# The decode state steps of a hybrid decoder kernel: products on ScalarE and VectorE instead of GpSimd

## The chip, the cores and the metric

The kernel runs on one core of a Trainium2 chip. The metric is the device time of one execution in microseconds (us), the median of several runs. The engines have short names in the profile: PE is TensorE (matrix products), PEld its weight loads, DVE is VectorE, ACT is ScalarE, POOL is GpSimd, and SP is the queue that issues the transfers (DMA).

## What is computed

The reference is one inference step of a two-layer decoder trunk, for a prompt of 1024 tokens and, with the same weights, for 8 samples of one new token each. Layer 0 has dilated attention and a state-space mixer (SSD) side by side, layer 1 is an mLSTM mixer. The change lies in the state-space mixer of the 8 samples, whose state is carried from token to token. For one new token the reference's scan comes down to this:

```python
state = state * exp(dt * a) + (dt * x) outer B      # (sample, head, 64, 128)
y     = sum over the last axis of state * C  +  d_skip * x
```

There are 8 samples, 16 heads, 64 values x per head and 128 state columns; B and C have 128 columns per group of heads. The new state is an output, and y goes on through a gate, a norm and the output projection.

## The kernel before

The kernel is written in a tile framework. The code issues instructions to the engines; the framework builds from it one queue per engine, and puts the semaphores in. The order within a queue follows from the dependences and the framework's own estimate of times, so it isn't always that of the code: in the profile both L840 of a step come before its first L842, and L747 of other work stands between the two L842. Once built, the order is fixed, and each engine works through its queue in order, waiting where it must.

All matrix products of the projections (`proj_c`, the matmuls of L112 into the PSUM tile `pf`) use a split of each float32 operand into a high and a low part: three matmuls for one. The weights arrive as `raw`, ScalarE makes the high part (L90, `wh`), VectorE the low one (L91, `wl`).

The stage around the change is the loop at L994 over the output tiles f of the layer's first projection. For f from 0 to 7 each tile belongs to the gate z, and is made in three column blocks c of 344 tokens: 24 matmuls, then `gate_c` takes the block out of PSUM (L235 a copy on ScalarE, L236 a tanh on ScalarE, L237 the product on VectorE), and it is stored to `zd`.

Two kinds of other work are put between these blocks:

- The prompt's state-space scan, in 16 units (chunk of 128 tokens x group). `ssd_prep` (L726 to L760) loads a tile of decays `sE` (L730) and `ea` (L738), masks `sE` with an affine select on GpSimd (L739), takes eight exponentials of 128x128 on ScalarE (L741) and one of `ea` (L743), makes a product and a transpose in the PSUM tile `pcb` (L745, L746), multiplies `sE` by it on VectorE (L747), copies the transpose to `sbt` on ScalarE (L749), transposes four tiles of x into `pxt` (L752) and scales them twice on VectorE (L758, L759). `ssd_main` makes `py` (L771), `pi` (L775) and `psl` (L777) on TensorE, updates the state on VectorE (L780 to L786) and the output on VectorE (L789) and GpSimd (L791). The PSUM tiles of these steps share a ring of five banks.
- The samples' decode steps, `dss_step(j)` (L829) for j from 0 to 7, one per f, called when the third block of a tile is done (the last ones, and what closes the sum, a little later). A step treats eight of the 64 values x of every head: 128 partitions are 8 samples x 16 heads, and the 1024 columns of the state tile `dst` are 8 values x 128 state columns. It loads the tile (L831), scales eight columns of x by dt on VectorE (L833, `dxd`), and then twice, for four values each: GpSimd makes x times B as one 128x512 product with broadcast operands into `dso` (L839), VectorE makes the new state from the old one (L840), GpSimd multiplies the new state by C into `dso` (L841), and VectorE sums each 128 columns (L842). Then the state is stored (L843).

The tiles `dso`, `gz` (the gate block) and `gth` (its tanh) come from one ring of four buffers. From f = 8 on the loop makes the attention gate, and the norm of the first half of the tokens begins.

Of the kernel before, what the change touches and what calls it, by code (L numbers as in the profile page):

```python
# [8 lines left out]
AF = mybir.ActivationFunctionType  # L9
# [19 lines left out]
def body(ctx, tc, I, O):  # L29
    nc = tc.nc  # L30
    V, A, G, PE = nc.vector, nc.scalar, nc.gpsimd, nc.tensor
    mult, add, sub, mx, mn = ALU.mult, ALU.add, ALU.subtract, ALU.max, ALU.min
# [23 lines left out]
    def S(name, dt=F32):  # L56
        return slab.tile([128, 1040], dt, tag="S", name=name)
# [7 lines left out]
    def SM(name, shape, bufs=2, dt=F32):  # L65
        return cur["sm"].tile(shape, dt, tag=name, name=name, bufs=bufs)
# [7 lines left out]
    def X(name="ax"):  # L74
        return ps.tile([128, 512], F32, tag="ax", name=name, bufs=8 - PS_MM)

    def TMP(name="tmp"):
        return tmpp.tile([128, 520], F32, tag="tmp", name=name)
# [4 lines left out]
    def C(name, shape, src=None, p=None):  # L83
        t = (p or cur["cst"]).tile(shape, F32, name=name)
        if src is not None:
            load(t, src)
        return t
# [27 lines left out]
    class Weights:  # L115
# [8 lines left out]
        def load(self, ahead=1):  # L124
            while len(self.raws) < min(ahead, len(self.srcs)):
                self.raws.append(raw_load(*self.srcs[len(self.raws)]))
# [152 lines left out]
    def conv_sample_act(t, y):  # L279
        A.activation(t, y, AF.Tanh)  # L280
        V.scalar_tensor_tensor(t, t, 1.0, y, add, mult)
        return t
# [212 lines left out]
    for g in range(4):  # L495
        for b in range(2):
            u = {}
# [201 lines left out]
    for f in range(12):  # L699
        w = wq0.next()  # L700
        raw = conv_raw()
        o = S("cout")
# [94 lines left out]
    B_b, C_b = BC_b[:, 0:128], BC_b[:, 128:256]  # L797
    dsc2 = C("dsc2", [128, 4])
# [30 lines left out]
    def dss_step(j):  # L829
        t = S("dst")  # L830
        load(t[:, :1024], I["sst"][:, j * 1024 : j * 1024 + 1024])  # L831
        xd = SM("dxd", [128, 8])
        V.tensor_scalar(xd, x_b[:, j * 8 : j * 8 + 8], dsc2[:, 0:1], None, mult)  # L833
        for u in range(2):
            o = TMP("dso")[:, :512]
            ov = o.rearrange("p (a b) -> p a b", b=128)
            tu = t[:, u * 512 : u * 512 + 512]
            tv = tu.rearrange("p (a b) -> p a b", b=128)
            G.tensor_tensor(ov, xd[:, 4 * u : 4 * u + 4].unsqueeze(2).broadcast_to([128, 4, 128]), B_b.unsqueeze(1).broadcast_to([128, 4, 128]), mult)  # L839
            V.scalar_tensor_tensor(tu, tu, dsc2[:, 1:2], o, mult, add)  # L840
            G.tensor_tensor(ov, tv, C_b.unsqueeze(1).broadcast_to([128, 4, 128]), mult)  # L841
            V.reduce_sum(y_b[:, j * 8 + 4 * u : j * 8 + 4 * u + 4], ov, AX.X)  # L842
        store(O["ssds"][:, j * 1024 : j * 1024 + 1024], t[:, :1024])  # L843

# [16 lines left out]

    dq.append(dss_prep)
    dq.extend(lambda j=j: dss_step(j) for j in range(8))
    dq.extend([dss_fin, dss_load, dss_fin2])

# [128 lines left out]
    for f in range(12):  # L994
# [11 lines left out]
        for c in range(3):  # L1006
            t = TMP("gz")
            c0 = c * CH
            if f >= 8:
                a = TMP("al")  # L1010
# [17 lines left out]
            if c < 2:  # L1028
                o = (f % 2) * 520 + c0
# [485 lines left out]
    for h in range(8):  # L1515
# [3 lines left out]
        for j in range(4):  # L1519
# [20 lines left out]
            o = S("cout")  # L1540
# [11 lines left out]
        for j in range(2):  # L1552
            w = wq1.next()
            t2 = S("msz")
            for c in range(3):
                gate_c(w, xh, xl, c, t2[:, c * CH : (c + 1) * CH])
                if j == 0 and c == 2:
                    t = conv_sample_act(*smp)
# [10 lines left out]
        for c in range(9):  # L1569
            vo_block(hd, c, wv)  # L1570
            if c == 1:
                p = X("pms")
# [291 lines left out]
```

## Time and profile before

| | us |
|---|---|
| median of 3 timed runs | 2150.44 (2147.65 to 2151.25) |
| the profiled execution | 2146.51 |
| its span, first to last instruction | 2144.6 |
| GpSimd busy in the 16 products L839, from 480 to 627 us | 18.9 |
| GpSimd busy in the 16 products L841, from 480 to 627 us | 23.8 |
| VectorE busy in the 16 updates L840 | 16.7 |
| VectorE busy in the 16 sums L842 | 10.9 |

A line of the timeline has the start in us, the length, the engine, the line of the kernel, the operation, the tile it writes and the tiles it reads, the shape, and how many instructions were merged into the line; in brackets stands how long the engine was idle before, and what released it. In the table by stage each row has a stretch of time, its length, the busy time of each engine with the number of instructions, the clock that TensorE was granted (1.00 is full), the share of the DMA engines' time, and GB/s. A releaser is inferred from semaphore events, and a wait for several is put down to the one that came last.

### The profile page before, as it was taken

To read this page: it belongs to the slowest core of one execution; us is meant where nothing else is said; L and a number is where in the kernel's file an instruction comes from. 1 tells how busy PE (TensorE), PEld (TensorE's weight loads), DVE (VectorE), ACT (ScalarE), POOL (GpSimd) and SP (SyncE) were. 2 spreads that over 40 slices of the span, in tenths; PEclk is the share of its full clock that TensorE was granted. 3 is DMA by queue.
4 is the path that set the end of the run, shared out by engine and by line. 5 is a ranking of instruction groups with operands and counts; after the bars stand their busy time and mean duration, and the time that the engine had idled before them with its cause. 6 is when DMAs were issued, how large, how long until landed. Compare 5 with 4: busy or idle time off the path is not lost.

```text
span 2144.6 us, 35154 instructions
## 1 busy us (share of the span) xinstructions
PE 2094.1 (98%) x12926; PEld 1878.8 (88%) x12926; DVE 1346.1 (63%) x3192; ACT 849.8 (40%) x1837; POOL 515.6 (24%) x1036
## 2 busy tenths in 40 slices
PE   7999999998899999999999999999999999999998
PEld 6877788997798899989989899898898998987798
DVE  7444378877877656555458466485664755756844
ACT  5434344544434334433335334253342433433421
POOL 4222100115440002152231421413215223141000
PEclk9999999999999999999999999999999999999999
DMA  4222053325555552411214133132231322406842
GB/s 161 73 73 78 21 155 104 96 92 168 157 187 183 174 173 64 100 31 54 84 40 161 28 100 115 35 129 64 91 125 31 102 94 68 151 22 208 280 164 95
DMA packets 162076, 232.29 MB, mean 108 GB/s; under 512 B 41200, under 2 KB 106976, under 8 KB 161904
## 3 DMA queue, kind: packets, MB, share of 16 engines
q1 hardware_dynamic: 161904, 230.04, 34.2%
q8 instruction: 102, 1.67, 0.3%
q14 instruction: 70, 0.57, 0.1%
HBM read 174.35 MB, written 55.62 MB: 107 GB/s over the span
## 4 chain that ended last, share of the span: by engine, by line
PE 78%; DVE 6%; DMA 3%; POOL 3%; issue 2%; ACT 2%; SPq 0%; POOLq 0%; DVEq 0%; ACTq 0%
PE pf L112 32%; PE pvo L112 16%; PE po L931 14%; PE pq L112 4%; PE mN L112 2%; PE mC L112 2%; PE pS L428 2%; PE pO L487 1%; PE mS L1294 1%; PE pT L470 1%; POOL mCl L91 1%; PE mH L1355 1%; PE mS L1296 1%; DMA mE<-mud 1%; POOL dso L841 1%
## 5 line engine op out<-in xcount | busy, mean ns | idle before, releaser
L112 PE MATMUL pf<-yh,wh 128*128 128x344 f32 x1152 | 370.2, 321 | 0.0
L112 PE MATMUL pf<-yl,wh 128*128 128x344 f32 x1152 | 368.9, 320 | 0.0
L112 PE MATMUL pf<-yh,wl 128*128 128x344 f32 x1152 | 368.5, 320 | 0.0
L91 DVE TENSOR_TENSOR wl<-raw,wh 128x1024 fp32r<-128x1024 f32 x128 | 159.8, 1248 | 148.2 <-ACT wh L90 147.8
L90 ACT CAST wh<-raw 128x1024 fp32r<-128x1024 f32 x128 | 133.9, 1047 | 252.8 <-PE po L931 101.0
L112 PEld LDWEIGHTS pf<-yh,wh 128*128 128x128 f32 x1152 | 216.9, 188 | 1.3 <-ACT craw L242 1.0
L112 PEld LDWEIGHTS pf<-yl,wh 128*128 128x128 f32 x1152 | 216.5, 188 | 0.0
L112 PEld LDWEIGHTS pf<-yh,wl 128*128 128x128 f32 x1152 | 216.4, 188 | 0.0
L112 PE MATMUL pvo<-wvh,yh 128*128 128x512 f32 x512 | 206.0, 402 | 0.0
L112 PE MATMUL pvo<-wvh,yl 128*128 128x512 f32 x512 | 201.9, 394 | 0.0
L112 PE MATMUL pvo<-wvl,yh 128*128 128x512 f32 x512 | 201.8, 394 | 0.0
L112 PE MATMUL pf<-xh,wh 128*128 128x344 f32 x576 | 194.3, 337 | 0.0
L112 PE MATMUL pf<-xl,wh 128*128 128x344 f32 x576 | 187.3, 325 | 0.0
L112 PE MATMUL pf<-xh,wl 128*128 128x344 f32 x576 | 187.3, 325 | 0.0
L1282 DVE TENSOR_SCALAR mx<-mx,mbs,md 128x256 f32<-128x256 f32 x64 | 26.4, 413 | 177.1 <-POOL md L1281 177.1
L250 DVE SCALAR_TENSOR_TENSOR cout<-craw,mcw,cout 128x1024 f32<-128x1024 f32 x96 | 123.0, 1282 | 13.2 <-ACT cout L248 11.7
L931 PE MATMUL po<-oh,wl 128*128 128x512 f32 (+2 forms) x384 | 122.9, 320 | 1.7 <-DVE wl L91 1.6
L931 PE MATMUL po<-oh,wh 128*128 128x512 f32 (+2 forms) x384 | 123.0, 321 | 0.9 <-ACT oh L90 0.9
L931 PE MATMUL po<-ol,wh 128*128 128x512 f32 (+2 forms) x384 | 123.0, 321 | 0.0
L112 PEld LDWEIGHTS pvo<-wvh,yl 128*128 128x128 f32 x512 | 96.1, 188 | 22.3
L112 PEld LDWEIGHTS pf<-xh,wh 128*128 128x128 f32 x576 | 110.1, 191 | 5.8 <-issue 5.4
L112 PEld LDWEIGHTS pvo<-wvh,yh 128*128 128x128 f32 x512 | 96.3, 188 | 20.8 <-issue 1.3
(440 smaller groups left out, 4995.5 us busy)
## 6 DMA issues: line engine op xcount, KB each, us to landing
raw<-in_wo SPq DMA_DIRECT2D x56, 512.0 KB
raw<-in_wq SPq DMA_DIRECT2D x32, 512.0 KB
raw<-in_wvo SPq DMA_DIRECT2D x32, 512.0 KB
dC<-in_mcs SPq DMA_DIRECT2D x32, 512.0 KB
out_mcs<-dC SPq DMA_DIRECT2D x32, 512.0 KB
raw<-in_wf SPq DMA_DIRECT2D x24, 512.0 KB
sE<-acd SPq DMA_DIRECT2D x16, 512.0 KB
raw<-in_wz SPq DMA_DIRECT2D x16, 512.0 KB
```

The source lines that it names most:

```text
L90: A.copy(hi, src)
L91: eng.tensor_tensor(lo, src, hi.bitcast(F32), sub)
L112: PE.matmul(out, l, r, start=i == 0, stop=i == n - 1)
L250: V.scalar_tensor_tensor(o[:, :NP], raw[:, j : j + NP], w4[:, j : j + 1], o[:, :NP], mult, add)
L428: PE.matmul(p[:, :n], qT[g][hs, qs], kT[g][hs, ks], start=True, stop=True)
L470: PE.transpose(pt[:, h * n + k : h * n + k + 128], P[:, k : k + 128], ident)
L487: PE.matmul(po[h * 64 : h * 64 + 64, qs], v, PT[:, h * n + k * 128 : h * n + k * 128 + 128], start=j + k == 0, stop=j == 7 and k == nk - 1)
L841: G.tensor_tensor(ov, tv, C_b.unsqueeze(1).broadcast_to([128, 4, 128]), mult)
L931: PE.matmul(p[:, :m], wt[:, ws], at, start=i == 0 and q == 0, stop=i == nk - 1 and q == 2)
L1282: V.tensor_scalar(x, x, bs[:, 6:7], d[:, 2:3], sub, mult)
L1294: PE.matmul(pS[:, 0:128], hd["k"][j][:, tok], hd["q"][j][:, tok], start=j == 0, stop=j == 1)
L1296: PE.transpose(pS[:, 128 + j * 128 : 256 + j * 128], hd["k"][j][:, tok], ident)
```

## The change

Only `dss_step` changes. The product of x and B is made by ScalarE, by four copies of 128x128 per half: each copies B with a scale per partition, one column of `dxd`. The product with C is made by VectorE in one 128x512 instruction. GpSimd has no part in the step any more. Buffers, loads, the state update, the sums and the store stay.

```diff
         for u in range(2):
             o = TMP("dso")[:, :512]
+            for i in range(4):
+                A.activation(o[:, i * 128 : i * 128 + 128], B_b, AF.Copy, scale=xd[:, 4 * u + i : 4 * u + i + 1])
+            tu = t[:, u * 512 : u * 512 + 512]
+            V.scalar_tensor_tensor(tu, tu, dsc2[:, 1:2], o, mult, add)
             ov = o.rearrange("p (a b) -> p a b", b=128)
-            tu = t[:, u * 512 : u * 512 + 512]
-            tv = tu.rearrange("p (a b) -> p a b", b=128)
-            G.tensor_tensor(ov, xd[:, 4 * u : 4 * u + 4].unsqueeze(2).broadcast_to([128, 4, 128]), B_b.unsqueeze(1).broadcast_to([128, 4, 128]), mult)
-            V.scalar_tensor_tensor(tu, tu, dsc2[:, 1:2], o, mult, add)
-            G.tensor_tensor(ov, tv, C_b.unsqueeze(1).broadcast_to([128, 4, 128]), mult)
+            V.tensor_tensor(ov, tu.rearrange("p (a b) -> p a b", b=128), C_b.unsqueeze(1).broadcast_to([128, 4, 128]), mult)
             V.reduce_sum(y_b[:, j * 8 + 4 * u : j * 8 + 4 * u + 4], ov, AX.X)
```

## The prediction

> **What bounds the kernel now.** I read the page of the profile first, then a table of the stage that holds the changed step (480 to 646 us), then its waits, then the order of time on each engine.
>
> ```profile
> PE 2094.1 (98%) x12926; PEld 1878.8 (88%) x12926; DVE 1346.1 (63%) x3192; ACT 849.8 (40%) x1837; POOL 515.6 (24%) x1036
> ...
> PE 78%; DVE 6%; DMA 3%; POOL 3%; issue 2%; ACT 2%; SPq 0%; POOLq 0%; DVEq 0%; ACTq 0%
> ```
>
> TensorE is the bound. An edit on the three other engines can move the end only where TensorE stands still because of them. So the question is how much TensorE loses in this stage, and to whom. Rows of the table by stage follow (stretch, its length, then the busy time of PE, PEld, DVE, ACT and POOL, the granted clock, the share and rate of DMA):
>
> ```profile
> 480.00:606.00 126.00, 114.57 (x801) 100.83 (x800) 101.91 (x180) 53.74 (x150) 67.72 (x87) 0.95 0.52 169
> ...
> 490.00:495.00 5.00, 4.85 (x39) 4.02 (x40) 5.00 (x12) 2.56 (x9) 1.75 (x4) 1.00 0.38 129
> ...
> 515.00:520.00 5.00, 4.45 (x20) 4.01 (x22) 5.00 (x11) 3.02 (x11) 1.74 (x4) 0.50 0.10 35
> ...
> 537.00:542.00 5.00, 4.79 (x25) 4.17 (x27) 5.00 (x12) 2.38 (x9) 1.28 (x4) 0.66 0.25 96
> ...
> 580.00:586.00 6.00, 4.36 (x19) 3.85 (x19) 6.00 (x13) 2.43 (x8) 2.37 (x4) 0.75 0.27 99
> ...
> 600.00:647.00 47.00, 45.58 (x300) 44.17 (x298) 35.46 (x61) 15.92 (x32) 15.44 (x17) 1.00 0.56 185
> ```
>
> TensorE is idle 126.00 - 114.57 = 11.4 us of the first stretch. The timeline of TensorE names the stops (start, length, instruction, and in brackets the idle time before it and its releaser):
>
> ```profile
> 490.15 0.63 PE L752 MATMUL pxt<-ident,cout 128*128 128x128 f32 x4 [1.69 <-DVE sx L759]
> ...
> 515.55 0.80 PE L745 MATMUL pcb<-cout 128*128 128x128 f32 x2 [3.10 <-ACT sbt L749]
> ...
> 537.17 0.49 PE L745 MATMUL pcb<-cout 128*128 128x128 f32 x2 [2.18 <-ACT sbt L749]
> ...
> 559.73 0.63 PE L752 MATMUL pxt<-ident,cout 128*128 128x128 f32 x4 [0.99 <-DVE sx L759]
> ...
> 580.65 0.49 PE L745 MATMUL pcb<-cout 128*128 128x128 f32 x2 [2.25 <-ACT sbt L749]
> ...
> 582.24 0.63 PE L752 MATMUL pxt<-ident,cout 128*128 128x128 f32 x4 [0.99 <-DVE sx L759]
> ```
>
> That is 11.2 of the 11.4 us. The stops come once per decode step: behind the steps 0, 1, 2, 3 and 4 of the eight. After the longer ones the granted clock drops: to 0.50, 0.66 and 0.75 in the rows above, while it stays at 1.00 after 1.69 us. In those three rows the low clock costs about 4.45 x 0.50 + 4.79 x 0.34 + 4.36 x 0.25 = 2.2 + 1.6 + 1.1 = 4.9 us more. So TensorE loses some 16 us behind five steps, the ceiling of what they can give back. How one step holds it, by step 2:
>
> ```profile
> 528.79 2.44 ACT L741 ACTIVATE sE<-sE,nacum 128x128 f32<-128x128 f32 x8
> ...
> 529.36 0.23 DVE L833 TENSOR_SCALAR dxd<-x_b,dsc 128x8 f32<-128x8 f32 x1
> ...
> 529.76 2.85 POOL L839 TENSOR_TENSOR dso<-dxd,BC_b 128x512 f32<-128x512 f32 x2 [1.63 <-DVE dxd L833]
> ...
> 531.65 2.17 DVE L840 SCALAR_TENSOR_TENSOR dst<-dst,dsc,dso 128x512 f32<-128x512 f32 x2 [0.93 <-POOL dso L839]
> ...
> 533.24 2.96 POOL L841 TENSOR_TENSOR dso<-dst,BC_b 128x512 f32<-128x512 f32 x2 [0.62 <-DVE dst L840]
> ...
> 535.00 0.69 DVE L842 TENSOR_REDUCE y_b<-dso 128x4 f32<-128x512 f32 x1 [1.18 <-POOL dso L841]
> 535.61 1.21 DVE L747 TENSOR_TENSOR sE<-sE,pcb 128x1024 f32<-128x1024 f32 x1
> ...
> 536.74 0.68 DVE L842 TENSOR_REDUCE y_b<-dso 128x4 f32<-128x512 f32 x1
> 536.85 0.27 ACT L749 COPY sbt<-pcb 128x128 f32<-128x128 f32 x1 [2.97 <-DVE sE L747]
> ```
>
> VectorE, in order, waits for GpSimd in the middle of the step. Behind that wait stands the multiplication of sE, behind it ScalarE's copy of sbt, and only that frees the PSUM bank for the next pcb. From GpSimd's start (529.76) to the end of the last reduction (537.42) the step holds VectorE 7.66 us, of which sE uses 1.13 (535.61 to 536.74): 6.5 us.
>
> **The change part by part.** The prices come from these rows and those above:
>
> ```profile
> 595.64 1.40 DVE L840 SCALAR_TENSOR_TENSOR dst<-dst,dsc,dso 128x512 f32<-128x512 f32 x2
> ...
> 496.40 1.09 POOL L739 TENSOR_SCALAR_AFFINE_SELECT sE<-sE 128x1024 f32<-128x1024 f32 x1 [2.29 <-DMA sE<-acd]
> ...
> 496.53 1.51 DVE L785 TENSOR_TENSOR ssdst<-ssdst,dec 128x512 f32<-128x512 f32 x1
> ...
> 539.55 0.68 DVE L785 TENSOR_TENSOR ssdst<-ssdst,dec 128x512 f32<-128x512 f32 x1
> ```
>
> Removed: four GpSimd operations of a step, 2.85 + 2.96 us in step 2. Added on ScalarE: eight scaled copies of 128x128. The row L741 gives eight of this shape in 2.44 us, 0.305 each; no row shows this copy itself, but the plain copy L749 took 0.27, so 2.2 to 2.44 per step, and I take 2.44. Added on VectorE: two products with C, each like the undisturbed L785, 0.68, of which the next instruction sees 0.6. No transfer is added or moved; the store of the state waits for the same two L840.
>
> A step after the change, counted from ScalarE's first copy: four copies, 4 x 0.305 and a little for the handover, 1.3 us; then on VectorE two L840 (1.4), two products (1.2) and two reductions (0.61 + 0.68, 1.3): 5.2, less about 0.1 where they overlap. The second four copies are ready at 2.5, before VectorE comes to them. So 5.1 us stand against 6.5, and **a step gains 1.4 us, less what ScalarE starts later than GpSimd did**. That delay is read from where ScalarE is busy:
>
> ```profile
> 479.65 0.46 ACT L236 ACTIVATE gth<-pf 128x344 f32<-128x344 f32 x1 [1.77 <-PE pda L676]
> ...
> 481.29 0.22 DVE L833 TENSOR_SCALAR dxd<-x_b,dsc 128x8 f32<-128x8 f32 x1
> ...
> 482.21 2.03 POOL L839 TENSOR_TENSOR dso<-dxd,BC_b 128x512 f32<-128x512 f32 x2
> ...
> 506.72 0.46 ACT L236 ACTIVATE gth<-pf 128x344 f32<-128x344 f32 x1
> ...
> 507.42 2.04 POOL L839 TENSOR_TENSOR dso<-dxd,BC_b 128x512 f32<-128x512 f32 x2
> ...
> 550.56 1.58 ACT L741 ACTIVATE sE<-sE,nacum 128x128 f32<-128x128 f32 x5
> ...
> 550.59 3.02 POOL L839 TENSOR_TENSOR dso<-dxd,BC_b 128x512 f32<-128x512 f32 x2 [1.41 <-DVE dxd L833]
> ...
> 570.16 0.47 ACT L236 ACTIVATE gth<-pf 128x344 f32<-128x344 f32 x1
> ...
> 574.05 2.04 POOL L839 TENSOR_TENSOR dso<-dxd,BC_b 128x512 f32<-128x512 f32 x2
> ```
>
> Step 0: ScalarE is free, xd is there at 481.5, GpSimd began at 482.21: 0.7 earlier, gain 2.1, but TensorE had only 1.7 to lose. Step 1: ScalarE free at 507.2 against 507.42, gain 1.6. Step 2: exponentials hold ScalarE until 531.23, 1.5 later than 529.76: nothing. Step 3: until 552.14, again 1.5 later: nothing. If the framework, which orders each engine's queue anew, puts the copies ahead of those exponentials, step 2 gives 1.4 and step 3 the 1.0 it has. Step 4: ScalarE is free at 570.6, GpSimd came at 574.05 because its affine select waited for a transfer: gain 4.8, of which TensorE has 2.25 + 0.99 = 3.2. Steps 5 to 7: TensorE's work covers them, 0; without the cover up to the 47.00 - 45.58 = 1.4 us idle in the last row. The sum is 1.7 + 1.6 + 0 + 0 + 3.2 = 6.5 us of idle TensorE. The stops of steps 1 and 4 get shorter than the 1.69 that left the clock alone, which would return 2.2 + 1.1 us; step 1's remainder of 1.5 is close to that mark, so I count half, 1.6. **Forecast: 8 us less.** What is late next is VectorE itself: 101.9 us busy in 126 before, plus 12 x 0.6, less what L840 loses today beside GpSimd (2.17 against 1.40 for two, 0.8 in each of five steps), about 105 in 118: not yet the bound.
>
> By the Trainium skill, page "TensorE: Matmul & The Clock Gate" (section "What's actually happening"), the array falls to half clock after an idle window of about 3.4 us. None of the stops is that long, so by the page alone no clock would return and the sum would be 6.5. The rows show 0.66 after a stop of 2.18, and the rows decide.
>
> **The rivals.** *The two engines collide.* GpSimd's affine select no longer stands behind the products and moves into the step, where VectorE now has two products more that read two SBUF operands. Beside an affine select (496.40 to 497.49), L785 took 1.51 instead of 0.68. One such meeting in each of five steps costs 5 x 0.83 = 4.2, leaving 4 of the 8 us: 2146.4. For it speaks this one row; against it that the removed products met L840 in most steps already. The Trainium skill, page "SBUF — State Buffer" (section "Who interferes with whom"), says that a VectorE instruction with two SBUF inputs contends with a GpSimd instruction that reads SBUF, and that the later one waits. By that rule the trace agrees: 1.51 against 0.68.
>
> *ScalarE's queue.* Slower than before:
>
> ```profile
> ACT sE L741 <- POOL sE L739: 29.5, 9, 7.0
> ```
>
> ScalarE stood still nine times, 3.3 us on average, because exponentials waited for an affine select. Copies queued behind such exponentials start that much later. A step loses from a delay of 1.4 us on; at 3.3 in all five steps it is 5 x 1.9 = 9.5 us, 2160. For it: step 2 and 3 are already at 1.5. Against it: in steps 0, 1 and 4 ScalarE ends its gate work before the next affine select, and that select is no longer held up by the products.
>
> *The copies go first.* Then steps 2 and 3 give 2.4 more and all three clock dips go: 11.2 idle less 1.5 and 0.8 that remain behind steps 1 and 2, plus 4.9, about 14 us, 2136.
>
> That the change does less than it says is not open: four GpSimd instructions per step go, whatever the order.
>
> **How the numbers follow.** The profiled execution took 2146.51 (span 2144.6), the median of the three timed runs is 2150.44; 8 us less gives 2138.5 and 2142.4. I forecast 2142.4. Chances: the forecast 0.49, copies first 0.13, collision 0.25, ScalarE's queue 0.13. A measurement of this kernel can tell about 0.2% from no change, here 4.3 us, so below 2146.1 is faster: 0.49 + 0.13 = 0.62. The collision lies within it: 0.25. Slower: 0.13. The range reaches from copies first with the 1.4 of the later steps (2150.44 - 14 - 1.4, 2135) to just above no change, 2152, which leaves out the queue and a little of the low end.
>
> **What the profile will show.** No GpSimd time on dso; L840 near 0.7 each; from the first copy to the last reduction about 5.1 us of VectorE without sE; TensorE's stops behind steps 0 and 4 gone, behind 1 about 1.5, behind 2 and 3 about as before; a clock near 1.00 around 515 and 580. Wrong would be: stops on TensorE that now begin at a copy of ScalarE, products of 1.5 us beside an affine select, or a stage of 126 us that keeps its length while VectorE is busy throughout.

## The result, and the profile after

| | before | after |
|---|---|---|
| median of the compared runs, us | 2149.22 (2147.65 to 2151.25, 4 runs) | 2129.12 (2126.93 to 2130.72, 4 runs) |
| span of the profiled execution, us | 2144.6 | 2128.5 |

The ratio is 0.991, with a 95% interval of 0.9897 to 0.9924: 20.1 us less by the medians, 16.3 to 22.1 by the interval. The kernel is faster, as forecast, but by more than twice the 8 us of the forecast, and below the range, which ended at 2135.

The page of the changed kernel has the same shape as before. First the busy times of the engines, then the shares of the chain that ended last:

```profile
PE 2088.0 (98%) x12926; PEld 1873.7 (88%) x12926; DVE 1348.8 (63%) x3208; ACT 869.3 (41%) x1901; POOL 478.0 (22%) x1004
...
PE 85%; DVE 4%; DMA 2%; POOL 2%; ACT 2%; issue 1%; SPq 0%; POOLq 0%; DVEq 0%; ACTq 0%
```

GpSimd has 32 instructions less, ScalarE 64 and VectorE 16 more, as the diff says. TensorE's share of the chain went from 78% to 85%: less of the end time is spent waiting for somebody else. The table by stage of the changed kernel, with the stretches that the prediction showed and one that spans all eight steps:

```profile
480.00:606.00 126.00, 125.32 (x913) 112.76 (x913) 118.86 (x218) 77.21 (x224) 44.99 (x67) 1.00 0.61 195
...
515.00:520.00 5.00, 5.00 (x45) 4.50 (x45) 5.00 (x11) 3.70 (x10) 1.70 (x4) 1.00 0.21 72
537.00:542.00 5.00, 5.00 (x35) 4.52 (x34) 5.00 (x12) 2.43 (x6) 2.02 (x4) 1.00 0.68 229
580.00:586.00 6.00, 6.00 (x48) 5.14 (x46) 5.62 (x9) 3.81 (x12) 1.62 (x2) 1.00 0.63 162
600.00:647.00 47.00, 47.00 (x308) 46.77 (x308) 39.90 (x81) 24.46 (x50) 3.00 (x4) 1.00 0.59 188
...
476.00:656.00 180.00, 178.94 (x1266) 164.93 (x1265) 165.58 (x309) 106.58 (x282) 48.99 (x73) 1.00 0.60 192
```

The same stretch of 180 us of the kernel before:

```profile
476.00:656.00 180.00, 166.97 (x1138) 151.33 (x1137) 142.28 (x257) 73.55 (x189) 83.52 (x102) 0.95 0.55 176
```

Before, TensorE was idle 180.00 - 166.97 = 13.0 us and lost about 166.97 x 0.05 = 8.3 us more to the lower clock, 21 us. After, it is idle 1.1 us, and the clock stays at 1.00: some 20 us come back in this stretch. The two executions shown here lie only 2144.6 - 2128.5 = 16.1 us apart, because outside the stretch the changed one loses more than the one before: 2.1 us more of idle time, and two dips of the granted clock, at 342 and at 1997 us, of 1.7 us each; 1.5 us stay unexplained. VectorE is busier in the stretch (165.58 against 142.28), in part because more of the program now fits into it, and TensorE does not suffer from that. Two of the waits of the changed kernel between 478 and 646 us (who waits, for whom, total us, times, longest):

```profile
DVE dst L839 <- ACT dso L837: 5.2, 6, 2.3
...
PE pcb L745 <- ACT sbt L749: 0.7, 1, 0.7
```

VectorE does wait for ScalarE's copies, up to 2.3 us at a time, but only 0.7 us of TensorE's time stands against that. How that comes about is seen in the order of time. Step 2 of the changed kernel (start, length, instruction), against the rows of the same step in the prediction:

```profile
524.69 1.56 ACT L741 ACTIVATE sE<-sE,nacum 128x128 f32<-128x128 f32 x5
...
525.96 1.21 DVE L91 TENSOR_TENSOR wl<-raw,wh 128x1024 fp32r<-128x1024 f32 x1
...
526.15 2.46 ACT L837 ACTIVATE dso<-BC_b,dxd 128x128 f32<-128x128 f32 x8
...
527.10 1.21 DVE L747 TENSOR_TENSOR sE<-sE,pcb 128x1024 f32<-128x1024 f32 x1
528.23 1.41 DVE L839 SCALAR_TENSOR_TENSOR dst<-dst,dsc,dso 128x512 f32<-128x512 f32 x2
...
528.51 0.25 ACT L749 COPY sbt<-pcb 128x128 f32<-128x128 f32 x1
...
529.55 1.28 DVE L841 TENSOR_TENSOR dso<-dst,BC_b 128x512 f32<-128x512 f32 x2
530.75 1.27 DVE L842 TENSOR_REDUCE y_b<-dso 128x4 f32<-128x512 f32 x2
```

Two things differ. The copies stand behind exponentials, as the forecast had it. But the multiplication of sE (L747), which stood between the two sums of the step, now stands ahead of the whole step: VectorE makes `wl` and sE while ScalarE copies. ScalarE's copy of `sbt`, which frees the bank for TensorE, comes at 528.51, in the middle of the step; before, it came at 536.85, 7.1 us after GpSimd had begun the step. The diff says nothing of L747. The framework estimated the changed step anew and built another order.

### The profile page after: what moved, and what is told of

Same layout as the page of the kernel before. It is cut to its first block, busy times and chain, and to the rows that moved or that the text cites. A ratio compares the mean times of both kernels' runs of the same rounds, so it can differ in the third digit from the quotient of the medians.

```text
span 2128.5 us, 35218 instructions
## 1 busy us (share of the span) xinstructions
PE 2088.0 (98%) x12926; PEld 1873.7 (88%) x12926; DVE 1348.8 (63%) x3208; ACT 869.3 (41%) x1901; POOL 478.0 (22%) x1004
## 4 chain that ended last, share of the span: by engine, by line
PE 85%; DVE 4%; DMA 2%; POOL 2%; ACT 2%; issue 1%; SPq 0%; POOLq 0%; DVEq 0%; ACTq 0%
PE pf L112 36%; PE pvo L112 16%; PE po L931 14%; PE pq L112 4%; PE mN L112 2%; PE mC L112 2%; PE pS L428 2%; PE pO L487 1%; PE mS L1294 1%; PE pT L470 1%; PE py L771 1%; POOL mCl L91 1%; PE mH L1355 1%; PE psl L777 1%; PE mS L1296 1%
## 5 line engine op out<-in xcount | busy, mean ns | idle before, releaser
L112 PEld LDWEIGHTS pvo<-wvl,yh 128*128 128x128 f32 x512 | 96.3, 188 | 20.0
```

The costliest lines, as they stand in the source:

```text
L112: PE.matmul(out, l, r, start=i == 0, stop=i == n - 1)
```

## The experiments

The two suspects were the engines (who makes the products) and the order (where L747 stands). In the short diffs, `issue_after` is the framework's means to hold an instruction back in its queue behind another one.

**1. The new order with the old engines.** GpSimd's x times B stays where it was; the rest of the step is issued behind the next unit's L747.

```diff
-        V.tensor_tensor(Ev, Ev, pc[:, 0:128]...)
+        e747 = V.tensor_tensor(Ev, Ev, pc[:, 0:128]...)
+        if "f" in dss_last:
+            with tc.issue_after(e747.ins):
+                dss_last.pop("f")()      # L840, L841, L842 and the store of the step
```

> The kernel before, with both products still on GpSimd; only the place of the step's VectorE work changes: the updates L840, GpSimd's products with C and the sums of a step are issued behind the next unit's multiplication of sE (L747), as they stand in the changed kernel, instead of ahead of it. Theory of the order (the gain is that L747 no longer waits behind the step in VectorE's queue, so that TensorE's pcb is freed): most of the 20 us appears, 2130 to 2138. Theory of the hold (the gain is that the step holds VectorE 5.1 us instead of 6.5, wherever L747 stands): the hold is that of before, 2146 to 2152.

Measured: 2142.26 against 2146.59 for before on the same chip, ratio 0.9978 (0.9966 to 0.999). Its row of the table by stage, from 476 to 656 us:

```profile
476.00:656.00 180.00, 169.84 (x1185) 154.77 (x1184) 152.35 (x271) 78.84 (x202) 85.80 (x104) 0.98 0.57 181
```

And its longest waits on VectorE and TensorE there:

```profile
DVE y_b L851 <- POOL dso L850: 9.4, 9, 1.2
PE pxt L756 <- DVE sx L763: 7.4, 5, 2.3
```

So order alone gives 4.3 us, which is neither of the two outcomes expected. TensorE's stop did not go, it moved: it now waits for the scalings sx, which stand behind a step that still waits for GpSimd (L850 and L851 are the product with C and the sum in this file).

**2. The new engines with the old order.** The changed kernel, with L747 held behind the step's first sum.

```diff
+        red = dss_last.pop("r", None)      # the first L842 of the step
+        with tc.issue_after(red) if red is not None else ExitStack():
+            V.tensor_tensor(Ev, Ev, pc[:, 0:128]...)
-        V.tensor_tensor(Ev, Ev, pc[:, 0:128]...)
```

> The changed kernel, with the one L747 that follows each step forced behind the step's first sum, where it stood in the kernel before; ScalarE and VectorE make the products. Theory of the order: most of the gain is lost, 2142 to 2150. Theory of the hold: the products' engines alone give it, 2127 to 2134. The recorded prediction's own arithmetic (order unchanged, engines changed) said 8 us less than before, about 2142.

Measured: 2138.18 against 2146.59, ratio 0.9961 (0.9947 to 0.9974): 8.4 us. The stops of its TensorE:

```profile
535.39 0.66 PE L755 MATMUL pxt<-ident,cout 128*128 128x128 f32 x4 [0.90 <-ACT sbt L752]
...
556.87 0.66 PE L755 MATMUL pxt<-ident,cout 128*128 128x128 f32 x4 [2.93 <-ACT sbt L752]
...
579.49 1.12 PE L755 MATMUL pxt<-ident,cout 128*128 128x128 f32 x4 [2.85 <-ACT sbt L752]
```

Again neither theory's range is met. With sE where the prediction had it, the kernel gains what the prediction said, 8 us. But the sum is right by luck in part: the stops behind steps 0 and 1 went (0.3 us is left), and those behind steps 3 and 4 are 2.9 us, where 0.99 and nothing were expected; the one behind step 2 is 0.90, where 2.18 was. Nor is the place of sE the whole reason for what is left. Here is step 3 (L750 is the multiplication of sE, L742 the exponentials, L752 the copy of `sbt` in this file):

```profile
550.55 1.21 DVE L750 TENSOR_TENSOR sE<-sE,pcb 128x1024 f32<-128x1024 f32 x1
...
555.68 0.99 ACT L742 ACTIVATE sE<-sE,nacum 128x128 f32<-128x128 f32 x3 [2.52 <-POOL sE L740]
556.57 0.24 ACT L752 COPY sbt<-pcb 128x128 f32<-128x128 f32 x1
```

sE was done at 551.76, but `sbt`, which TensorE waits for, was copied only 4.8 us later: it stood in ScalarE's queue behind exponentials of the next unit, and these waited for GpSimd's affine select. Behind step 4 it is the same, 4.1 us. So forcing the place of one VectorE instruction changed ScalarE's queue as well, and the 8.4 us are not the price of the engines at an order that is otherwise that of before.

**3 and 4. Half of the change each.** First x times B on ScalarE with C left to GpSimd, then C on VectorE with x times B left to GpSimd.

```diff
+            for i in range(4):
+                A.activation(o[:, i * 128 : i * 128 + 128], B_b, AF.Copy, scale=xd[:, 4 * u + i : 4 * u + i + 1])
-            G.tensor_tensor(ov, xd[:, 4 * u : 4 * u + 4]..., B_b..., mult)
```

> Only the product with B goes to ScalarE, the product with C stays on GpSimd. The framework then puts L747 ahead of the step by itself from step 1 on. Theory of the order: 2128 to 2138, nearly the whole gain, although VectorE still waits for GpSimd's product with C. Theory of the hold: half of the gain or less, 2138 to 2146.

```diff
-            G.tensor_tensor(ov, tv, C_b..., mult)
+            V.tensor_tensor(ov, tv, C_b..., mult)
```

> Only the product with C goes to VectorE, the product with B stays on GpSimd. The framework leaves L747 behind the whole step here. Theory of the order: little gain, 2141 to 2150. Theory of the hold: the longer of the two GpSimd products is gone, about half of the gain, 2135 to 2142.

Measured: 2136.71 (ratio 0.9958, 0.9943 to 0.9973) and 2137.1 (0.9962, 0.9952 to 0.9973) against 2146.59, so 9.9 and 9.5 us. The same row of the first:

```profile
476.00:656.00 180.00, 173.55 (x1211) 159.22 (x1211) 151.99 (x278) 99.83 (x271) 65.32 (x87) 0.98 0.59 183
```

And of the second:

```profile
476.00:656.00 180.00, 172.97 (x1215) 158.21 (x1215) 163.02 (x293) 81.39 (x205) 67.35 (x87) 0.99 0.57 183
```

Each half gives half, and each time the other theory fits: the 2136.71 of the first lies in the range of the order, the 2137.1 of the second in that of the hold. They also tell which half turns the order: with x times B on ScalarE the framework puts L747 ahead of the step; with C alone moved it stays behind, here behind both sums of steps 1 to 5.

**5 to 7. TensorE's order.** The changed kernel's TensorE queue is another one as well: behind a step, matmuls of the next gate block stand between `pcb` and `pxt`, so that TensorE has something to do while VectorE is late. Is that the cause? First the kernel before with the plain gate block directly behind the step, then the changed kernel with all gate matmuls held behind the unit's `pxt`, and as its control the kernel before with the same hold.

```diff
-            own = f < 8 and (c < 2 or f < 2)
+            own = f < 8 and (c > 0 or f < 2)
```

> The kernel before, both products on GpSimd; from tile f = 2 on the two scan units of a tile stand in the second and third gate block instead of the first and second, so that TensorE has a plain block of 24 gate matmuls right behind each decode step, as the framework's new order gives it in the changed kernel. Theory of TensorE's order (the larger part of the gain is that TensorE has gate matmuls to do while the step holds VectorE): 8 to 16 us less than before, though GpSimd still makes the products. Theory of the engines (the products' engines and the place of L747 are all): no gain, within 3 us of before.

```diff
+                with tc.issue_after(pinned[-1]) if pinned else ExitStack():
                     PE.matmul(out, l, r, start=i == 0, stop=i == n - 1)
...
+        pinned.append(pt_.ins)      # the unit's last L752
```

> The changed kernel with TensorE's queue held to the order of the kernel before around each step: the transposes pxt of a unit come right behind its pcb and ahead of every later gate matmul. Theory of TensorE's order: the gain falls to that of the engines alone, 5 to 10 us less than before (the recorded 8). Theory of the engines: 15 to 20 us less, as in the changed kernel.

> Control: the kernel before (GpSimd) with the same hold on TensorE's queue. That queue stands nearly so already from the third step on; both theories: 0 to 5 us slower than before. The difference between this kernel and the pinned changed kernel is what the engines give at one order of TensorE: by the recorded arithmetic about 8 us.

Measured, against 2146.41: 2146.93 for the other gate block (ratio 1.0001, 0.9991 to 1.001); 2141.61 for the changed kernel held (0.9973, 0.9961 to 0.9985); 2157.25 for the control (1.0053, 1.0038 to 1.0068). The first shows no gain, as the theory of the engines had it; the held kernel comes out just short of the range of the other theory, and the control is 10.8 us slower, where 0 to 5 were expected. The held changed kernel, ahead of the steps and in them:

```profile
0.00:476.00 476.00, 448.78 (x2845) 380.68 (x2845) 295.83 (x827) 208.60 (x569) 88.02 (x205) 0.99 0.31 91
476.00:656.00 180.00, 176.55 (x1245) 161.39 (x1244) 156.52 (x297) 100.03 (x277) 44.15 (x72) 1.00 0.59 185
```

The control:

```profile
0.00:476.00 476.00, 448.99 (x2829) 380.28 (x2829) 294.07 (x827) 207.45 (x565) 87.33 (x205) 0.99 0.31 91
476.00:656.00 180.00, 167.63 (x1140) 150.46 (x1140) 138.70 (x238) 73.09 (x197) 84.22 (x101) 0.95 0.52 165
```

Read alone, the middle figure would say that TensorE's order is worth three quarters of the gain, since only 4.8 us remain of 20. The control shows why that reading is wrong: the hold costs 10.8 us in the old kernel too. It bears on all scan units, and the price falls mostly ahead of the first step (TensorE busy 448.8 and 449.0 up to 476 us; the changed kernel without the hold is busy 456.1 there). Between the two held kernels lie 2157.25 - 2141.61 = 15.6 us, and in the steps the held one is idle 3.5 us at full clock, against 12.4 at 0.95 for its control (whose rows are from the slowest of its four executions, 2162.5). With TensorE's order forced, most of the gain stands.

**8. All on VectorE.** No ScalarE and no GpSimd; the framework leaves L747 behind the step, here behind both sums.

```diff
-            G.tensor_tensor(ov, xd[:, 4 * u : 4 * u + 4]..., B_b..., mult)
+            V.tensor_tensor(ov, xd[:, 4 * u : 4 * u + 4]..., B_b..., mult)
...
-            G.tensor_tensor(ov, tv, C_b..., mult)
+            V.tensor_tensor(ov, tv, C_b..., mult)
```

> Both products on VectorE, none on ScalarE or GpSimd: 16 products more of about 0.6 us on VectorE than in the changed kernel, no wait for another engine. The framework puts 33 to 46 gate matmuls of TensorE ahead of the pcb behind a step. Theory of TensorE's order: with that cover the gain stays at 10 to 17 us. Theory of the engines: L747 stands behind the whole step and the hold is 5.1 us of VectorE's own work, so like the run with L747 forced behind, about 8 us or less.

Measured: 2150.64 against 2146.41, ratio 1.0015 (1.0005 to 1.0026), slower by 4.2 us. Its step 2 on VectorE:

```profile
529.15 1.81 DVE L839 TENSOR_TENSOR dso<-dxd,BC_b 128x512 f32<-128x512 f32 x2
530.89 1.60 DVE L840 SCALAR_TENSOR_TENSOR dst<-dst,dsc,dso 128x512 f32<-128x512 f32 x2
532.42 1.28 DVE L841 TENSOR_TENSOR dso<-dst,BC_b 128x512 f32<-128x512 f32 x2
533.62 1.26 DVE L842 TENSOR_REDUCE y_b<-dso 128x4 f32<-128x512 f32 x2
534.81 1.20 DVE L747 TENSOR_TENSOR sE<-sE,pcb 128x1024 f32<-128x1024 f32 x1
```

No wait on another engine is left in the step, 5.7 us from 529.15 to 534.81, and still nothing is gained; neither theory had it slower. sE comes behind all of it and is done at 536.01. But that is not what ends TensorE's stop behind the step:

```profile
538.61 0.63 ACT L743 ACTIVATE ea<-ea 128x512 f32<-128x512 f32 x1 [2.60 <-DMA ea<-acd]
...
542.23 0.25 ACT L749 COPY sbt<-pcb 128x128 f32<-128x128 f32 x1
...
542.53 0.80 PE L745 MATMUL pcb<-cout 128*128 128x128 f32 x2 [3.85 <-ACT sbt L749]
```

The copy of `sbt` came 6.2 us after sE, because in ScalarE's queue it stood behind exponentials and a cast, and these behind a transfer of `ea`. All five stops at `pcb` of this run (12.9 us) end with such a copy, 2.4 to 6.2 us after sE; in step 2 of the kernel before it followed sE at once (536.82, 536.85). So this loss is that of a new order of two queues. That ScalarE's making of the products is what counts was one reading of this run; run 10 puts that to the test.

**9. GpSimd, with still more ahead.** As in 1, but both scalings sx (L758, L759) ahead of the step too.

```diff
-        V.tensor_tensor(xw, pxv, wl[:, gi]...)
+        e759 = V.tensor_tensor(xw, pxv, wl[:, gi]...)
+        if "f" in dss_last:
+            with tc.issue_after(e759.ins):
+                dss_last.pop("f")()
```

> GpSimd keeps both products, but VectorE takes the next unit's multiplication of sE and both scalings sx ahead of the step's update and sums. Theory 1 (what the step holds up on VectorE is what matters, by whichever engine it waits for): TensorE no longer waits for sE or sx behind a step, so most of the loss goes, 12 to 17 us less than before. Theory 2 (the place alone does little, the engine must be quicker too): as with sE alone ahead, about 5 us less, because what now stands behind the sums (the gate product gz, the update of ssdst) waits for GpSimd in its turn.

**10. All on VectorE, with sE ahead.** The eight instructions of 8, issued behind the next L747 by the means of 1.

```diff
+            with tc.issue_after(e747.ins):
+                dss_last.pop("f")()      # both products, the updates, the sums and the store
```

> VectorE makes both products, and takes the next unit's multiplication of sE ahead of all eight instructions of the step. Theory 1 (order decides): the step holds VectorE 5.4 us without a wait and sE is not behind it, so 10 us or more less than before. Theory 2 (ScalarE's share of the work decides): VectorE has 1.2 us more per step than in the changed kernel and sx stands behind it, so the time stays near that of all on VectorE with sE behind, 2150, within 3 us of before.

**11. The changed kernel as it is**, on the chip of 9, 10 and 12.

> The changed kernel as it is, for the same chip and the same runs of before as the other three. Both theories: 16 to 22 us less than before, TensorE idle about 1 us between 476 and 656 us.

**12. The changed kernel with sx ahead as well**: the edit of 9 on the changed kernel.

> The changed kernel with both scalings sx ahead of the step as well, not sE alone. If the changed kernel has given back all that the steps cost TensorE (1.1 us of idle time left in 476 to 656), this is within 3 us of it, about 20 us less than before. If something of the steps' cost is left that the count of idle time does not show, it is 3 us or more below the changed kernel.

Measured, all against 2145.5: 9 took 2139.78 (ratio 0.9972, 0.9961 to 0.9982), 10 took 2132.41 (0.9939, 0.9926 to 0.9952), 11 took 2127.12 (0.9919, 0.9906 to 0.9932), 12 took 2126.93 (0.9914, 0.99 to 0.9927). For 9, the second theory holds: 5.7 us. Its step 2 on VectorE:

```profile
530.33 1.40 DVE L849 SCALAR_TENSOR_TENSOR dst<-dst,dsc,dso 128x512 f32<-128x512 f32 x2
532.91 0.69 DVE L851 TENSOR_REDUCE y_b<-dso 128x4 f32<-128x512 f32 x1 [1.17 <-POOL dso L850]
533.51 0.98 DVE L237 SCALAR_TENSOR_TENSOR gz<-gth,gz 128x344 f32<-128x344 f32 x1
...
535.01 0.67 DVE L784 TENSOR_TENSOR ea<-pi,ea 128x512 f32<-128x512 f32 x1
```

And the stop of its TensorE behind step 1:

```profile
517.90 1.09 PE L775 MATMUL py<-sE,sx 128*64 128x128 f32 x16 [1.41 <-DVE ea L784]
```

Whatever is put behind GpSimd's products waits for them: first sE, in 1 sx, here gz and ea, and TensorE stops at `py` in place of `pxt`. For 10, the first theory holds, and the reading of run 8 falls: VectorE alone gains 13.1 us once sE stands ahead. Step 2 of 10 on VectorE:

```profile
528.38 1.20 DVE L748 TENSOR_TENSOR sE<-sE,pcb 128x1024 f32<-128x1024 f32 x1
529.51 1.28 DVE L845 TENSOR_TENSOR dso<-dxd,BC_b 128x512 f32<-128x512 f32 x2
530.71 2.29 DVE L846 SCALAR_TENSOR_TENSOR dst<-dst,dsc,dso 128x512 f32<-128x512 f32 x2
```

The same eight instructions, the updates even slower (2.29 against 1.60), but sE is done at 529.58 in place of 536.01, and `sbt` is copied at 529.61 in place of 542.23. And 12 has nothing left to give. Its stretch by stage:

```profile
476.00:656.00 180.00, 180.00 (x1271) 166.17 (x1271) 166.09 (x309) 106.53 (x282) 46.70 (x73) 1.00 0.61 192
```

TensorE is never idle in it, and the time is that of 11 within 0.2 us. No version is faster than the changed kernel by more than can be measured. Together, in us against before on the same chip:

| who makes the products | sE behind a sum (in run 8 behind both) | sE ahead of the step | difference, with all that the framework moved |
|---|---|---|---|
| GpSimd both | 0 (before) | -4.3 (run 1) | 4.3 |
| ScalarE x times B, VectorE C | -8.4 (run 2) | -18.4 (run 11) | 10.0 |
| VectorE both | +4.2 (run 8) | -13.1 (run 10) | 17.3 |

Engines with the old place of sE give 8.4, the new place with the old engines 4.3, both 18.4: more than the sum. The rows above suggest the reason. With GpSimd in the chain something on VectorE stands behind the wait; with sE behind the step, the step's own 4 to 6 us and what ScalarE puts ahead of `sbt` stand before TensorE's bank is free. This is a reading, and the table is no clean separation: in runs 2 and 8 ScalarE's queue changed too, as shown, and run 4, with sE behind both sums and GpSimd still making x times B, gains 9.5. What is shown is that the same engines differ by 10.0 and 17.3 us with the order of the queues.

## Why the prediction was wrong

*TensorE is the bound, and the gain is the loss it has behind the steps*: right. Idle time and clock between 476 and 656 us account for 21 - 1 = 20 us, and the medians differ by 20.1. That these agree so closely is luck in part, since the two executions that the rows come from differ by 16.1.

*The ceiling of some 16 us*: too low, though not the failed step. It was summed over 480 to 606 us, and it took too little for the clock there. The granted clock of a row is a mean over its stretch, and two of the prediction's rows end before the dips do: in rows of 1 us the clock is at 0.50 until 521.5, 542.0 and 586.4, and the three dips cost 3.0 + 1.7 + 1.7 = 6.4 us in place of 4.9. The first of them, in the kernel before:

```profile
515.00:521.00 6.00, 5.45 (x30) 4.94 (x30) 6.00 (x13) 3.22 (x11) 1.74 (x4) 0.50 0.08 29
```

The rest stands in one place further on:

```profile
644.00:651.00 7.00, 5.40 (x32) 5.09 (x31) 5.18 (x18) 3.73 (x7) 1.93 (x2) 0.77 0.48 137
```

Idle 1.6 us, and 1.7 us of clock (0.50 from 647.8 to 651.2). The text counted the 1.4 us of idle time as a possible extra and no clock for it; it took steps 5 to 7 for covered. In the changed kernel this stop is gone.

*"A step gains 1.4 us, less what ScalarE starts later than GpSimd did"*: this is the step that failed. The price of the step was right. Its copies take 2.46, the two updates 1.41, the two products 1.28 and the sums 1.27, all within 0.1 of the estimates. What failed is the rule that the step's length is what TensorE waits for. It held only as long as sE stands behind the step, and the text took this for fixed. From 1.5 us of delay it concluded *"nothing"* for steps 2 and 3; in truth sE of step 2 went ahead and came 1.5 us after the step's `dxd` in place of 6.2 (527.10 - 525.62 against 535.61 - 529.36), so that neither the delay nor the length of the step mattered. Run 2 forces the prediction's premise, and gives 8.4 us, with other stops than the prediction's; run 11 without it gives 18.4. So about 10 us of the gain come from an order that the prediction had taken as given.

*"If the framework, which orders each engine's queue anew, puts the copies ahead"*: the text saw that the queues are built anew, and asked it of one queue only. The copies did stay behind the exponentials in steps 1 to 4. It was VectorE's queue that changed (and TensorE's with it), and the text did not ask what VectorE would do in the time in which it now had to wait for ScalarE's first copies.

*The clock returns by half, 1.6 us*: all 8 us of it in these 180 us returned, since no long stop was left.

*The rivals.* The collision took place. These are the rows of the tile `dso` in the changed kernel (shortest, median, longest in ns):

```profile
L837 ACT ACTIVATE dso<-BC_b,dxd x64: 386/391/407, 484.1 to 603.2; 128x128 f32<-128x128 f32 x64
L839 DVE SCALAR_TENSOR_TENSOR dst<-dst,dsc,dso x16: 741/750/1449, 485.8 to 604.4; 128x512 f32<-128x512 f32 x16
L841 DVE TENSOR_TENSOR dso<-dst,BC_b x16: 676/685/1577, 487.9 to 605.6; 128x512 f32<-128x512 f32 x16
```

The longest L839 and L841 are 0.7 and 0.9 us above the median, once in step 0 and once in step 1, each beside an affine select of GpSimd (at 485.97 and 511.04); behind these two TensorE had other work. In step 2 an affine select met a product as well, but there the product had begun 0.08 us earlier (529.55) and kept its time; the affine select took 2.16 us, where an undisturbed one takes 1.09:

```profile
529.63 2.16 POOL L739 TENSOR_SCALAR_AFFINE_SELECT sE<-sE 128x1024 f32<-128x1024 f32 x1 [2.14 <-DMA sE<-acd]
```

The Trainium skill, page "SBUF — State Buffer" (section "Who interferes with whom"), has both engines share an interface for such operands; by that rule the trace agrees, 1577 against 685 ns. ScalarE's queue also delayed the copies as that rival said, 2.3 us at the most on VectorE, and cost TensorE no more than the 0.7 us above. *The copies go first* was nearest in size, for another reason than the true one.

What stays open: how much of the order's share is the place of sE, and how much that of `sbt` in ScalarE's queue, since no run held both. The loss counted between 476 and 656 us is good to 2 to 5 us as a measure of time. In run 9 it falls by some 11 us (idle 8.4 and 1.7 of clock are left), and the time by 5.7. Why the framework's estimate turned the order was not tried; runs 3 and 4 show only that x times B on ScalarE does it.

## What to carry to other kernels

Where a framework orders the queues, a change of engine is two changes: the price of the work, and a new order of everything around it; cost the step with its neighbours ahead of it and behind it, on every engine that it touches, and let the range reach to the better of the two. A chain that goes back and forth between two engines costs the one that has other work to do more than its busy time, because all that stands behind each wait is late. And an experiment that forces an order needs the same force on the old kernel beside it: run 6 without run 7 would have named the wrong cause. Even then the other queues have to be read again: in runs 2 and 8 it was ScalarE's that held TensorE up.

## What the runs showed of the hardware

Of the 21 us that TensorE lost in the kernel before, 8 were not idle time but clock. Here is run 1, after its stop of 2.35 us that ended at 518.19:

```profile
519.00:520.00 1.00, 1.00 (x14) 0.79 (x15) 1.00 (x4) 0.11 (x1) 0.00 (x0) 0.83 0.48 176
520.00:523.00 3.00, 3.00 (x17) 2.67 (x14) 3.00 (x7) 0.27 (x1) 1.75 (x4) 0.50 0.35 113
523.00:524.00 1.00, 1.00 (x7) 0.79 (x7) 1.00 (x4) 0.00 (x0) 0.00 (x0) 0.96 0.60 197
```

In rows of 1 us, all 20 dips between 476 and 656 us, in all runs, are of this form: the clock goes to 0.50 and stays there for 3.4 us, or for twice that, and values between are rows in which a dip begins or ends. The length does not follow that of the stop: 3.4 us after the 2.93 of run 2, 6.8 after the 3.10 of the kernel before. So a dip costs 1.7 us of work or 3.4, often as much as the stop itself.

Most single stops up to 1.9 us left the granted clock at 1.00 (1.81 in run 1, 1.76 and 1.79 in run 3, 1.91 in run 4), 15 of the 16 from 2.15 us on went with a dip (2.15 in run 4, 2.35 in run 1). The bound is not sharp on either side: the one exception is run 5, where a stop of 2.73 us, up to 623.82, left the clock at 1.00; and in the kernel before a stop of 1.60 us between two runs of tiny matmuls (eight of 8x8, eight of one column) was followed by the dip at 647.8. The Trainium skill, page "TensorE: Matmul & The Clock Gate" (section "What's actually happening"), gives an idle window of about 3.4 us; these traces show a drop after two thirds of that.

A scaled copy of 128x128 with a scale per partition (L837), not seen before the change, lasts 386 to 407 ns, and in a row of eight one follows the other every 0.30 us ((2.46 - 0.39) / 7), as the exponentials of this shape do (2.44 us for eight).
